# Two-layer hybrid trunk: delta-rule and retention heads issued in steps, with projections advanced K block by K block between them

## The chip, the cores and the metric

One core of one Trainium2 chip runs the whole program. The metric is device microseconds for one execution. Order on each engine is fixed when the program is built: TensorE, VectorE, ScalarE, GpSimd and the queue of SP (which issues nearly all DMAs) each work through their own list, and wait on semaphores for one another.

## The reference: what is computed

There are 512 latent tokens, 256 context tokens, a width of 2048 and two layers. In float32, each layer does the following:

```python
h  = rmsnorm(x, norm_w) * (1 + scale) + shift      # scale, shift, gate from silu(c) @ ada_w + ada_b
z  = h @ w_in                                      # one projection, split by columns
ret = silu(z_rg) * rmsnorm(retention(rope(z_rq), rope(z_rk), z_rv))       # 4 heads of 128, both directions
q, k, v = silu(conv5(z_q, z_k, z_v));  q, k = l2norm(q), l2norm(k)
gdn = silu(z_gg) * rmsnorm(gated_delta_rule(q, k, v, g, beta))            # 4 heads of 128, both directions
mla = silu(z_mg) * attention(z_cq, z_ckv, z_kr)                           # 8 heads, low-rank q and kv
x  = x + gate * (concat(ret, gdn, mla) @ w_out)
```

The context tokens go through the same weights and read only context. In the second layer their output isn't needed, so most projections there are for the latents alone. The delta rule works on six chunks of 128 tokens per head and direction: a triangular inverse per chunk, then a chain of six dependent steps that carries a 128x128 state.

## The kernel before, in words

Each layer has three phases. Phase A projects the normalised input (tiles `hs`, 16 K blocks, each as a high and a low fp32r part) into all branches and runs the delta-rule and retention heads. Phase B is the attention, phase C the output projection with the residual.

A projection of 128 columns (`proj`, L290) loads its weights in tiles of four K blocks (`load_w`, tile `raw`, 5 buffers), splits them on ScalarE (`wh`, L227) and VectorE (`wl`, L228; 4 buffers each) and runs three matmuls of 512 latent columns into PSUM tile `zl` per K block, and three of 256 context columns into `zc` where the context is needed. PSUM tag "z" has three buffers. `ada_job` runs once in the middle of a projection: it advances the modulation vectors for later, with products on ScalarE (`ada_p`, L470) and sums on GpSimd (`ada_a`, L472).

What comes after a projection is of several kinds. `gate` (L614) applies SiLU and stores to DRAM (`gate_d`, L621), `latent` (L625) stores the attention's compressed inputs, `ret_raw` and `ret_v` (L942, L950) store retention's q, k and v (`ret_d`), and `conv_in` (L733) does the five-tap convolution on VectorE (L747) and SiLU, and leaves its result in a tile for the head.

`gdn_head` (L752) does, in order: project and convolve q, its sums of squares (L763); project and convolve k, turn it to token order (`knp`, L657), normalise, turn back (`ktp`); project and convolve v, turn it (`vnp`); decays `et` and `es`; the chunks' inverses by rounds of small float16 matmuls and VectorE operations (L841 to L891); the chain of six steps in both directions (L900 to L938); `out_norm` (L666). The work tiles come from shared tags, among them "t" with five buffers and "h" with five.

`ret_head` (L968) loads a retention head's q, k, v, applies the rotary tables, builds decay tables, and goes over six chunks: scores, a multiplication on VectorE, a split, and a weighted sum into `racc` (L1033).

A list of all other projections (`fill`, L1052) is cut in eight (`nf`), and each piece is traced behind one head. The tile framework orders each engine's instructions by a planning run with modelled durations: whatever is ready, the one traced first goes first; weight loads and splits are traced with high priority. So projections traced behind a head stand, in TensorE's list, in the gaps that the plan sees in the head.

```python
            fill = cq + gg[1:2] + ckv + gg[2:3] + rr[0] + gg[3:] + rr[1] + rr[2] + rr[3] + mg
            nf = [7, 6, 4, 5, 3, 3, 4, 4]
            for i, n in enumerate(nf):
                (gdn_head if i < 4 else ret_head)(*((i, gs) if i < 4 else (i - 4,)))
                for f in fill[sum(nf[:i]):sum(nf[:i + 1])]:
                    f()
```

The first four projections of a layer (`C_KR` and q, k, v of delta head 0) are done earlier by `first_groups` and only picked up in phase A.

Of the kernel before, what the change touches and what calls it, by code (L numbers as in the profile page):

```python
# [44 lines left out]
RSCALE = 1024.0  # L45

# [55 lines left out]
def trunk(  # L102
# [206 lines left out]

    FIRST = (C_KR, C_GDN, C_GDN + 512, C_GDN + 1024)  # L310
# [41 lines left out]
    def pair_groups(l, cols, hs, need_ctx):  # L352
# [54 lines left out]
    ret_d = [[[dr.tile([P, NT], F32, name=f"ret_d{l}_{h}_{w}") for w in range(3)] for h in range(4)] for l in range(DEPTH)]  # L407
    g_d = [dr.tile([48, P], F32, name=f"g_d{l}") for l in range(DEPTH)]
# [194 lines left out]
    def phase_a(l, hs):  # L603
        last = l == DEPTH - 1
        parB = par[l, 1]
        if True:
# [7 lines left out]
            def gate(c0, j):  # L614
                lo_ctx = not last
                zl, zc = proj_in(l, (c0), hs, lo_ctx)
# [8 lines left out]
            def latent(c0, j, need_ctx):  # L625
                kind = 0 if j < 6 else 1
                zl, zc = proj_in(l, (c0), hs, need_ctx)
# [38 lines left out]
            def out_norm(o, lo, wcol, j, fill_v=mean_eps):  # L666
# [5 lines left out]
                scale_tokens(sq, o, r, c0)  # L672
                m = pm("ot")
# [5 lines left out]
            def kr_ab():  # L679
                zl, zc = proj_in(l, C_KR, hs, True)  # L680
# [52 lines left out]
            def conv_in(dst, c0, grp, need_ctx):  # L733
                zl, zc = proj_in(l, c0, hs, need_ctx)
# [4 lines left out]
                w = lambda j: parB[:, 12 * j + grp:12 * j + grp + 1]  # L739
# [10 lines left out]
                silu_mul(dst[:, lo:NT], y[:, lo:NT], e[:, lo:NT])  # L750

            def gdn_head(h, gs):  # L752
                be, gcol, egl, ekd, nbe = gs
                qT = pt("qT")
                qlo = NX if last else 0
                conv_in(qT, C_GDN + h * P, h, not last)
                qv = tiny("qv")
                sq = mk("lsq")
                S.activation(out=sq[:, qlo:NT], in_=qT[:, qlo:], func=AF.Square)
                m = pm("ss")  # L760
                c0 = qlo // P
                for n in range(c0, NCH):
                    T.matmul(m[:, n:n + 1], lhsT=sq[:, n * P:(n + 1) * P], rhs=ones[:, 0:1], start=True, stop=True)  # L763
                V.tensor_scalar(out=qv[:, c0:], in0=m[:, c0:NCH], scalar1=EPS, scalar2=EPS * HD, op0=ALU.add, op1=ALU.mult)
                kr = mk("kr")
                conv_in(kr, C_GDN + 512 + h * P, 4 + h, True)
# [5 lines left out]
                m = pm("ktp")  # L772
                turn(m, kn, 0)
                S.copy(kT, m[:, :NT])
                vT = mk("vT")
                conv_in(vT, C_GDN + 1024 + h * P, 8 + h, True)
                if h == 0:
                    gate(C_GDN + 1536, 4)

# [4 lines left out]
                S.copy(vn, m[:, :NT])  # L784
                on = pt("on")
                qch = range(2, NCH) if last else range(NCH)
# [50 lines left out]
                for n_ in range(5):  # L837
# [7 lines left out]
                    else:  # L845
# [525 lines left out]
```

## Time and profile before

| | us |
|---|---|
| median of 3 runs | 3240.17 (3236.0 to 3242.21) |
| profiled execution, first to last instruction (its span; no other time of it is given) | 3227.6 |
| TensorE busy | 3066.9 |
| VectorE busy | 2026.6 |
| ScalarE busy | 1643.0 |
| GpSimd busy | 695.7 |

The profile is of one execution. Times in its views are microseconds from the first instruction. PE is TensorE, PEld its weight loads, DVE VectorE, ACT ScalarE, POOL GpSimd; `SPq` is SP's queue. L763 is line 763 of the kernel. A matmul's recorded duration overlaps the next one's, so the distance between starts tells the rate. PEclk is the granted clock of TensorE: 1.00 is 2.4 GHz, and in a stretch's mean a lower figure is a share of time at 1.2 GHz. Phase A of layer 0 lies at about 200 to 1300 us, that of layer 1 at about 1960 to 2800; delta head 1 of layer 0 lies at about 440 to 660.

### The profile page before, as it was taken

The numbers are of one execution on the slowest core, as the hardware profiler recorded it, in microseconds if no ns is written. First come the engines' busy times: TensorE is split into PE (matmuls) and PEld (weight loads), VectorE is DVE, ScalarE is ACT, GpSimd is POOL, SyncE is SP. The second block draws the span as 40 slices with busy tenths as digits, with TensorE's granted clock in tenths as the row PEclk, the third lists the DMA queues.
The fourth block names the chain that finished last, engine by engine and source line by source line (L and its number), as shares of the span: only waits on it lengthen the run. The fifth ranks groups of instructions, "written<-read, shape, count | busy, mean of one in ns | idle before, by whom it ended". The sixth has DMA issues, their size and how long they took to land.

```text
span 3227.6 us, 50779 instructions
## 1 busy us (share of the span) xinstructions
PE 3066.9 (95%) x18925; PEld 2583.6 (80%) x18925; DVE 2026.6 (63%) x3524; ACT 1643.0 (51%) x3492; POOL 695.7 (22%) x487
## 2 busy tenths in 40 slices
PE   7998988989989999999999998899999999999998
PEld 3466877878778878899888887688898888888887
DVE  3259558568577666666743266867585767766634
ACT  3256555554654666544665566442425235644533
POOL 0026344444442554000246503200000000000000
PEclk9999999989999999999999999999999999999999
DMA  9763333433424555511465443321423256512444
GB/s 308 217 198 111 113 111 93 130 87 92 123 86 134 154 162 159 159 48 50 141 208 152 142 112 108 108 72 55 108 58 95 75 152 178 153 51 64 133 118 128
DMA packets 496654, 399.22 MB, mean 124 GB/s; under 512 B 45366, under 2 KB 433046, under 8 KB 496406
## 3 DMA queue, kind: packets, MB, share of 16 engines
q1 hardware_dynamic: 496310, 395.95, 41.5%
q8 instruction: 148, 2.42, 0.3%
q14 instruction: 100, 0.82, 0.1%
q0 software_dynamic: 96, 0.02, 0.0%
HBM read 340.90 MB, written 54.97 MB: 123 GB/s over the span
## 4 chain that ended last, share of the span: by engine, by line
PE 58%; DVE 4%; ACT 3%; issue 1%; DMA 1%; POOL 0%; SPq 0%; ACTq 0%; DVEq 0%; POOLq 0%
PE zl L284 20%; PE zlc L284 10%; PE zc L286 5%; PE vz L267 4%; PE sc L1153 3%; PE zlc L286 2%; PE oacc L1212 2%; PE zt L275 2%; PE ptp L1205 1%; PE racc L1033 1%; PE f L284 1%; DVE wl L228 1%; DVE cy L747 1%; ACT ada_p L470 0%; PE chain L912 0%
## 5 line engine op out<-in xcount | busy, mean ns | idle before, releaser
L472 POOL TENSOR_TENSOR ada_a<-ada_a,ada_p 128x512 f32<-128x512 f32 x480 | 693.8, 1445 | 1355.0 <-ACT ada_p L470 1259.7
L228 DVE TENSOR_TENSOR wl<-raw,wh 128x512 fp32r<-128x512 f32 x632 | 471.2, 753 | 198.2 <-ACT wh L227 155.3
L284 PE MATMUL zl<-hh,wh 128*128 128x512 f32 (+1 forms) x1440 | 584.9, 407 | 6.4 <-ACT wh L227 2.9
L284 PE MATMUL zl<-hh,wl 128*128 128x512 f32 (+1 forms) x1440 | 583.0, 405 | 6.6 <-DVE wl L228 6.6
L284 PE MATMUL zl<-hl,wh 128*128 128x512 f32 (+1 forms) x1440 | 584.6, 406 | 1.0 <-DVE hl L228 1.0
L470 ACT ACTIVATE ada_p<-araw,const_f 128x256 f32<-128x256 f32 x960 | 422.9, 499 | 86.9 <-DMA araw<-in_ada_w_dram 57.2
L227 ACT CAST wh<-raw 128x512 fp32r<-128x512 f32 x632 | 368.7, 601 | 72.8 <-PE vz L267 18.2
L284 PEld LDWEIGHTS zl<-hh,wh 128*128 128x128 f32 (+1 forms) x1440 | 275.2, 191 | 75.0 <-issue 9.1
L284 PEld LDWEIGHTS zl<-hh,wl 128*128 128x128 f32 (+1 forms) x1440 | 275.2, 191 | 67.6 <-DVE wl L228 8.1
L284 PEld LDWEIGHTS zl<-hl,wh 128*128 128x128 f32 (+1 forms) x1440 | 275.8, 192 | 63.5 <-DVE hl L228 4.2
L286 PE MATMUL zc<-hh,wh 128*128 128x256 f32 (+1 forms) x960 | 279.6, 291 | 3.2 <-ACT ce L372 1.8
L286 PE MATMUL zc<-hh,wl 128*128 128x256 f32 (+1 forms) x960 | 279.0, 291 | 0.0
L286 PE MATMUL zc<-hl,wh 128*128 128x256 f32 (+1 forms) x960 | 278.5, 290 | 0.0
L286 PEld LDWEIGHTS zc<-hh,wh 128*128 128x128 f32 (+1 forms) x960 | 184.2, 192 | 12.5 <-issue 4.7
L286 PEld LDWEIGHTS zc<-hl,wh 128*128 128x128 f32 (+1 forms) x960 | 184.4, 192 | 6.9 <-issue 5.0
L286 PEld LDWEIGHTS zc<-hh,wl 128*128 128x128 f32 (+1 forms) x960 | 184.1, 192 | 5.1 <-issue 4.6
L284 PE MATMUL zlc<-mh,wl 128*128 128x512 f32 x448 | 176.7, 395 | 0.0
L284 PE MATMUL zlc<-mh,wh 128*128 128x512 f32 x448 | 175.8, 392 | 0.0
L284 PE MATMUL zlc<-ml,wh 128*128 128x512 f32 x448 | 175.4, 391 | 0.0
L747 DVE SCALAR_TENSOR_TENSOR cy<-cz,const_f,cy 128x511 f32<-128x511 f32 (+3 forms) x176 | 145.7, 882 | 28.0 <-ACT cy L740 27.7
L284 PEld LDWEIGHTS zlc<-mh,wh 128*128 128x128 f32 x448 | 84.1, 188 | 19.0 <-issue 1.2
L284 PEld LDWEIGHTS zlc<-ml,wh 128*128 128x128 f32 x448 | 84.0, 187 | 18.3
(1250 smaller groups left out, 6426.0 us busy)
## 6 DMA issues: line engine op xcount, KB each, us to landing
raw<-in_w_in_dram SPq DMA_DIRECT2D x368, 256.0 KB, 3.7
araw<-in_ada_w_dram SPq DMA_DIRECT2D x256, 256.0 KB, 3.2
raw<-in_w_out_dram SPq DMA_DIRECT2D x144, 256.0 KB, 4.1
ar<-in_ada_w_dram SPq DMA_DIRECT2D x128, 256.0 KB, 4.8
x_d<-xt SPq DMA_DIRECT2D x32, 384.0 KB, 5.4
raw<-in_w_in_dram SPq DMA_DIRECT2D x72, 128.0 KB, 3.2
ret_d<-rw SPq DMA_DIRECT2D x20, 384.0 KB, 4.0
rz<-ret_d SPq DMA_DIRECT2D x20, 384.0 KB, 4.3
```

What stands on the lines that cost most here:

```text
L227: S.copy(hi, src)
L228: V.tensor_tensor(out=lo, in0=src, in1=hi.bitcast(F32), op=ALU.subtract)
L267: T.matmul(z[:, 256 * i:256 * i + 256], lhsT=x_[:, (j + i) * P:(j + i + 1) * P], rhs=w, start=first and k == 0 and i == 0, stop=end and k ...
L275: T.matmul(z, lhsT=w, rhs=xx[:, a:b], start=own and first and k == 0, stop=own and last and k == nk - 1)
L284: T.matmul(zl[:m], lhsT=w, rhs=xx[:, NX:], start=st, stop=sp)
L286: i = T.matmul(zc[:m, :NX], lhsT=w, rhs=xx[:, :NX], start=st and zc_open, stop=sp and zc_open)
L470: S.activation(out=pr[:, v], in_=raw[:, i, :], func=AF.Copy, scale=cs32[:, 2 * k + v:2 * k + v + 1])
L472: G.tensor_tensor(out=acc, in0=acc, in1=pr, op=ALU.add)
L747: V.scalar_tensor_tensor(out=y[:, a_:b_], in0=z[:, a_ + o:b_ + o], scalar=w(j), in1=y[:, a_:b_], op0=ALU.mult, op1=ALU.add)
L1033: T.matmul(acc[:, :NL], lhsT=a[:, sl], rhs=b[:, :NL], start=st and i == 0, stop=sp and i == NCH - 1)
L1153: T.matmul(m[:, po:po + n], lhsT=a[:, qs], rhs=b[:, ko:ko + n], start=i == 0, stop=i == len(ops) - 1)
L1212: T.matmul(acc[:, os], lhsT=a[:, sl], rhs=b[:, js], start=j == 0 and n == 0, stop=j == nk - 1 and n == 2)
```

## The change

Projections of phase A become tasks: Python generators that trace one K block and then give back its length in microseconds (`STEP_US`; 2.1 for `ret_v`). `pump(us)` inside `gdn_head`, `ret_head` and `out_norm` advances the first unfinished tasks by that much, so that these matmuls are traced between the steps of the head, ahead of the head's next step. `need(key)` advances the list until all tasks of a key are done. Weights are taken four K blocks at a time. The convolutions of a delta head (`conv_task`) become tasks as well, placed one head ahead in the list, in the order k, v, q; their results are stored in DRAM (`conv_d`) and loaded by `gdn_load` ahead of the previous head's output norm. Inside a head, the two directions are traced step by step side by side. The number of projections, taps and `ada_job` calls is the same.

```diff
+STEP_US = (0.7, 1.05)
...
+    def proj_steps(segs, xs, m, need_ctx):
+        nk = len(xs)
+        zl = pz("zl")
+        zc = pz("zc") if need_ctx else None
+        for k0 in range(0, nk, 4):
+            ws = load_w(segs, k0, 4, m)
+            for j in range(4):
+                pmm(ws[j:j + 1], xs, k0 + j, nk, m, zl, zc)
+                yield STEP_US[bool(need_ctx)]
+            if k0 == 4:
+                ada_job()
+        return zl, zc
...
-    def pair_groups(l, cols, hs, need_ctx):
...
+                yield 4 * STEP_US[bool(need_ctx)]
...
-        return proj(segs, hs, m, need_ctx, True)
+        return (yield from proj_steps(segs, hs, m, need_ctx))
...
+                pump(6)
...
+                zl, zc = ready.pop((l, C_KR))
...
+            def conv_task(h, which):
+                need = which > 0 or not last
+                zl, zc = yield from proj_in(l, C_GDN + 512 * which + h * P, hs, need)
                 z = ev("cz")
-                lo = 0 if need_ctx else NX
...
-                silu_mul(dst[:, lo:NT], y[:, lo:NT], e[:, lo:NT])
-
-            def gdn_head(h, gs):
+                silu_mul(z[:, lo:NT], y[:, lo:NT], e[:, lo:NT])
+                dma(out=conv_d[l][h][which][:, lo:], in_=z[:, lo:])
+
+            def gdn_load(h):
+                qlo = NX if last else 0
+                kr, vT, qT = mk("kr"), mk("vT"), pt("qT")
+                for w, t in ((1, kr), (2, vT), (0, qT)):
+                    lo = qlo if w == 0 else 0
+                    dma(out=t[:, lo:], in_=conv_d[l][h][w][:, lo:])
+                return kr, vT, qT
+
+            def gdn_head(h, gs, loaded, pump):
...
-                conv_in(kr, C_GDN + 512 + h * P, 4 + h, True)
+                qch = range(2, NCH) if last else range(NCH)
+                kr, vT, qT = loaded
...
-                if h == 0:
-                    gate(C_GDN + 1536, 4)
-
+                pump(4)
...
+                qv = tiny("qv")
+                sq = mk("lsq")
+                S.activation(out=sq[:, qlo:NT], in_=qT[:, qlo:], func=AF.Square)
+                pump(4)
+                m = pm("ktp")
+                turn(m, kn, 0)
+                S.copy(kT, m[:, :NT])
+                pump(2)
+                ss = pm("ss")
+                for n in qch:
+                    T.matmul(ss[:, n:n + 1], lhsT=sq[:, n * P:(n + 1) * P], rhs=ones[:, 0:1], start=True, stop=True)
+                V.tensor_scalar(out=qv[:, c0:], in0=ss[:, c0:NCH], scalar1=EPS, scalar2=EPS * HD, op0=ALU.add, op1=ALU.mult)
...
+                pump(4)
...
+                pump(4)
...
+                pump(8)
...
+                        pump(1)
...
+                    pump(3)
...
+                    ms = []
...
+                        ms.append(vt)
+                        pump(1)
+                    for d in both:
                         mx = pm("xp")
                         for sl in sls:
-                            T.matmul(mx[:, sl], lhsT=X[d][:, sl], rhs=vt[:, sl], start=True, stop=True)
+                            T.matmul(mx[:, sl], lhsT=X[d][:, sl], rhs=ms[d][:, sl], start=True, stop=True)
                         V.tensor_tensor(out=Xt[d], in0=Xt[d], in1=mx[:, :NT], op=ALU.subtract)
+                        pump(1)
...
+                        pump(1)
...
+                pump(2)
...
+                    if step:
+                        pump(1)
+                    for d, (n, cl, sl) in enumerate(info):
+                        T.matmul(pp[d][:, P:2 * P], lhsT=Xs[d][:, sl], rhs=rs[d], start=True, stop=True)
...
+                    pump(1)
+                    S2 = [None] * 2
+                    for d, (n, cl, sl) in enumerate(info):
...
+                    pump(1)
+                ahead = gdn_load(h + 1) if h < 3 and need("conv", h + 1) else None
                 out_norm(on, qlo, parB[:, 71:72], 4 + h, lambda ss: V.scalar_tensor_tensor(
-                    out=ss, in0=ss, scalar=1.0 / HD, in1=qv[:, c0:], op0=ALU.mult, op1=ALU.add))
+                    out=ss, in0=ss, scalar=1.0 / HD, in1=qv[:, c0:], op0=ALU.mult, op1=ALU.add), pump)
+                return ahead
...
-                    for j, z in enumerate(zs):
-                        tok_mm(z, hs, ws, 2 * j, k0, KD)
+                    for i in range(4):
+                        for j, z in enumerate(zs):
+                            tok_mm(z, hs, ws[i:i + 1], 2 * j, k0 + i, KD)
+                        yield 2.1
...
+                pump(8)
...
+                    pump(3)
...
+                pump(2)
                 m = pm("on")
                 turn(m, o, qlo // P)
-                out_norm(m, qlo, parB[:, 70:71], h)
-
+                out_norm(m, qlo, parB[:, 70:71], h, pump=pump)
...
+            tasks = {}
+
+            def task(name, g):
+                tasks[name] = g
+
+            def advance(name):
+                us = next(tasks[name], None)
+                if us is None:
+                    del tasks[name]
+                return us or 0
+
+            def pump(us):
+                while us > 0 and tasks:
+                    us -= advance(next(iter(tasks)))
+
+            def need(*key):
+                while any(n[:len(key)] == key for n in tasks):
+                    pump(0.1)
+                return True
+
+            def pair_gate(j):
+                yield from pair_steps(l, (C_MG + j * P, C_MG + (j + 1) * P), hs, not last)
+                for i in (j, j + 1):
+                    yield from gate(C_MG + i * P, 8 + i)
+
+            conv = lambda h: [task(("conv", h, w), conv_task(h, w)) for w in (1, 2, 0)]
+            cq = lambda a, b: [task(("cq", j), latent(C_CQ + j * P, j, not last)) for j in range(a, b)]
+            ckv = lambda a, b: [task(("ckv", j), latent(C_CKV + j * P, 6 + j, True)) for j in range(a, b)]
+            gg = lambda h: task(("gg", h), gate(C_GDN + 1536 + h * P, 4 + h))
+            rr = lambda h: [task(("rr", h, w), ret_raw(h, w)) for w in range(2)]
+            rv = lambda h: task(("rr", h, "v"), ret_v(h))
+            rg = lambda h: task(("rr", h, "g"), gate(C_RET + 1536 + h * P, h))
+            mg = lambda a, b: [task(("mg", j), gate(C_MG + j * P, 8 + j)) for j in range(a, b)]
             gs = kr_ab()
-            cq = [lambda j=j: latent(C_CQ + j * P, j, not last) for j in range(6)]
-            ckv = [lambda j=j: latent(C_CKV + j * P, 6 + j, True) for j in range(4)]
-            rr = [[lambda h=h, w=w: ret_raw(h, w) for w in range(2)] +
-                  [lambda h=h: ret_v(h)] * (1 - h % 2) + [lambda h=h: gate(C_RET + 1536 + h * P, h)] for h in range(4)]
-            gg = [lambda h=h: gate(C_GDN + 1536 + h * P, 4 + h) for h in range(4)]
-            mg = [lambda j=j: gate(C_MG + j * P, 8 + j) for j in range(8)]
-            mg.insert(6, lambda: pair_groups(l, (C_MG + 6 * P, C_MG + 7 * P), hs, not last))
-            fill = cq + gg[1:2] + ckv + gg[2:3] + rr[0] + gg[3:] + rr[1] + rr[2] + rr[3] + mg
-            nf = [7, 6, 4, 5, 3, 3, 4, 4]
-            for i, n in enumerate(nf):
-                (gdn_head if i < 4 else ret_head)(*((i, gs) if i < 4 else (i - 4,)))
-                for f in fill[sum(nf[:i]):sum(nf[:i + 1])]:
-                    f()
+            conv(0)
+            need("conv", 0)
+            gg(0)
+            cq(0, 6)
+            conv(1)
+            gg(1)
+            ckv(0, 4)
+            conv(2)
+            gg(2)
+            rr(0)
+            rv(0)
+            conv(3)
+            gg(3)
+            rg(0)
+            rr(1)
+            rg(1)
+            rr(2)
+            rv(2)
+            rg(2)
+            rr(3)
+            rg(3)
+            mg(0, 6)
+            task(("mg", 6), pair_gate(6))
+            ahead = gdn_load(0)
+            pump(24)
+            for h in range(4):
+                need("gg", h)
+                ahead = gdn_head(h, gs, ahead, pump)
+            for h in range(4):
+                need("rr", h)
+                if h % 2:
+                    need("rr", h - 1)
+                ret_head(h, pump)
+            while tasks:
+                pump(1)
```

## Rows read from the trace of the kernel before

**Rows 1.** Profile page: the span, and busy time of each engine.

```profile
span 3227.6 us, 50779 instructions
...
PE 3066.9 (95%) x18925; PEld 2583.6 (80%) x18925; DVE 2026.6 (63%) x3524; ACT 1643.0 (51%) x3492; POOL 695.7 (22%) x487
```

**Rows 2.** Busy time by stretch, layer 0; columns in the first line.

```profile
core 0: us, PE busy (x) PEld busy (x) DVE busy (x) ACT busy (x) POOL busy (x), PEclk, DMA share, GB/s
200.00:440.00 240.00, 214.96 (x1395) 182.26 (x1395) 173.35 (x266) 145.58 (x327) 116.74 (x79) 0.96 0.45 134
440.00:510.00 70.00, 55.70 (x298) 47.64 (x296) 47.72 (x69) 42.89 (x91) 28.70 (x20) 0.90 0.24 66
660.00:730.00 70.00, 57.05 (x317) 49.45 (x316) 46.70 (x66) 39.39 (x85) 27.08 (x20) 0.88 0.25 72
880.00:950.00 70.00, 58.32 (x331) 49.44 (x331) 54.15 (x87) 43.11 (x95) 34.44 (x23) 0.91 0.21 61
440.00:1040.00 600.00, 537.98 (x3679) 466.66 (x3678) 410.76 (x655) 332.16 (x753) 248.64 (x174) 0.95 0.35 101
1040.00:1300.00 260.00, 248.61 (x1473) 213.91 (x1471) 174.02 (x221) 168.09 (x366) 122.06 (x82) 0.99 0.55 161
200.00:1300.00 1100.00, 1001.55 (x6542) 862.82 (x6541) 758.12 (x1140) 645.83 (x1444) 487.44 (x334) 0.96 0.42 123
1300.00:1600.00 300.00, 299.70 (x1955) 269.97 (x1953) 203.38 (x401) 151.19 (x307) 12.33 (x10) 1.00 0.31 91
```

**Rows 3.** Busy time by stretch, phase A of layer 1.

```profile
1960.00:2060.00 100.00, 82.50 (x400) 64.61 (x399) 82.70 (x138) 68.15 (x151) 44.27 (x30) 0.90 0.43 116
2060.00:2800.00 740.00, 735.00 (x4783) 627.57 (x4782) 514.47 (x982) 309.98 (x626) 0.00 (x0) 1.00 0.37 106
```

**Rows 4.** Waits of TensorE, 440:1040, largest first: us, times, longest.

```profile
PE knp L657 <- DVE kr L400: 15.9, 3, 5.6
PE ss L763 <- ACT lsq L759: 15.5, 3, 5.3
PE vtp L848 <- DVE vt L842: 8.0, 4, 2.9
PE ot L657 <- DVE osq L660: 4.7, 2, 3.3
```

**Rows 5.** Timeline of TensorE, 443:453: start, us, operation, idle before.

```profile
442.82 0.40 PE L284 MATMUL zl<-hl,wh 128*128 128x512 f32 x1
...
443.88 0.40 PE L284 MATMUL zl<-hl,wh 128*128 128x512 f32 x1
449.27 2.72 PE L763 MATMUL ss<-const_f,lsq 128*128 128x1 f32 x12 [4.99 <-ACT lsq L759]
...
452.20 0.63 PE L284 MATMUL zl<-hh,wl 128*128 128x512 f32 x1
```

**Rows 6.** Groups of VectorE by line, 200:1300; count, busy us, mean ns.

```profile
L228 DVE TENSOR_TENSOR wl<-raw,wh 128x512 fp32r<-128x512 f32 x180 | 166.5, 926 | 54.7 <-ACT wh L227 41.4 <-issue 7.3 <-POOL ada_a L472 3.5
L747 DVE SCALAR_TENSOR_TENSOR cy<-cz,const_f,cy 128x254 f32<-128x254 f32 (+1 forms) x96 | 92.4, 1022 | 10.7 <-ACT cy L740 10.7
```

**Rows 7.** Groups of VectorE by line, 2060:2800.

```profile
L228 DVE TENSOR_TENSOR wl<-raw,wh 128x512 fp32r<-128x512 f32 (+1 forms) x170 | 114.7, 680 | 28.9 <-ACT wh L227 28.7
L747 DVE SCALAR_TENSOR_TENSOR cy<-cz,const_f,cy 128x510 f32<-128x510 f32 (+3 forms) x60 | 35.3, 638 | 15.5 <-ACT cy L740 15.2
```

**Rows 8.** DMA issues on the page: count, KB, us to landing.

```profile
ret_d<-rw SPq DMA_DIRECT2D x20, 384.0 KB, 4.0
rz<-ret_d SPq DMA_DIRECT2D x20, 384.0 KB, 4.3
```

**Rows 9.** Waits of SP's queue, the largest.

```profile
SPq L621 <- DVE gz L400: 181.3, 24, 17.7
```

**Rows 10.** Busy time by stretch, head 1 of layer 0.

```profile
498.00:605.00 107.00, 95.76 (x743) 81.56 (x743) 81.76 (x154) 55.20 (x132) 42.81 (x30) 0.98 0.32 92
440.00:660.00 220.00, 197.20 (x1301) 168.38 (x1300) 144.59 (x228) 125.51 (x283) 95.88 (x67) 0.96 0.36 104
```

More of the change, by code (lines that the diff above doesn't have):

```diff
@@ L407, in trunk @@
     ret_d = [[[dr.tile([P, NT], F32, name=f"ret_d{l}_{h}_{w}") for w in range(3)] for h in range(4)] for l in range(DEPTH)]
+    conv_d = [[[dr.tile([P, NT], F32, name=f"conv_d{l}_{h}_{w}") for w in range(3)] for h in range(4)] for l in range(DEPTH)]
     g_d = [dr.tile([48, P], F32, name=f"g_d{l}") for l in range(DEPTH)]
@@ L615, in gate @@
                 lo_ctx = not last
-                zl, zc = proj_in(l, (c0), hs, lo_ctx)
+                zl, zc = yield from proj_in(l, c0, hs, lo_ctx)
                 z, e = ev("gz"), ev("ge")
@@ L626, in latent @@
                 kind = 0 if j < 6 else 1
-                zl, zc = proj_in(l, (c0), hs, need_ctx)
+                zl, zc = yield from proj_in(l, c0, hs, need_ctx)
                 e = ev("ce")
@@ L876, in gdn_head @@
                 for it in range(2):
+                    Rs = []
                     for d in both:
@@ L899, in gdn_head @@
                 small = lambda name, tag, bufs: wk.tile([P, P], F32, name=name, tag=tag, bufs=bufs)
+                pump(2)
                 for step in range(NCH):
-                    for d in both:
-                        n, cl, end = orders[d][step], col(d), step == NCH - 1
-                        sl = sls[n]
-                        p_ = pc("chain") if d == 0 else pm("chain")[:, :512]
+                    end = step == NCH - 1
+                    info = [(orders[d][step], col(d), sls[orders[d][step]]) for d in both]
+                    pp, rs, vd, vnew = [None] * 2, [None] * 2, [None] * 2, [None] * 2
+                    for d, (n, cl, sl) in enumerate(info):
+                        pp[d] = pc("chain") if d == 0 else pm("chain")[:, :512]
@@ L905, in gdn_head @@
                         if step == 0:
[L906 removed]
+                            rs[d] = vn[:, sl]
                         else:
[L908 to L910 removed]
+                            T.matmul(pp[d][:, 0:P], lhsT=kT[:, sl], rhs=St[d], start=True, stop=True)
@@ L919, in gdn_head @@
-                            S.copy(vnew, p_[:, P:2 * P])
+                            vnew[d] = small("vnew", "svn", 2)
+                            S.copy(vnew[d], pp[d][:, P:2 * P])
+                    pump(1)
+                    S2 = [None] * 2
+                    for d, (n, cl, sl) in enumerate(info):
                         if not end:
-                            T.matmul(p_[:, 2 * P:3 * P], lhsT=kn[:, sl], rhs=vd, start=True, stop=True)
-                            S2 = small("St", "ss", 4)
+                            T.matmul(pp[d][:, 2 * P:3 * P], lhsT=kn[:, sl], rhs=vd[d], start=True, stop=True)
+                            S2[d] = small("St", "ss", 4)
@@ L944, in ret_raw @@
                 lo = 0 if need else NX
-                zl, zc = proj_in(l, C_RET + 512 * which + h * P, hs, need)
+                zl, zc = yield from proj_in(l, C_RET + 512 * which + h * P, hs, need)
                 z = ev("rw")
@@ L966, in ret_v, with ret_head @@
                     dma(out=ret_d[l][h + e][2], in_=o)
-            def ret_head(h):
+            def ret_head(h, pump):
                 qlo = NX if last else 0
@@ L1059, in phase_b @@
+            for h in range(4):
[4 more added lines that the diff above has]
+            while tasks:
+                pump(1)
     def phase_b(l):
```

58 lines of the change are left out of this document (20 added, 38 removed).

## The prediction

> **What bounds the kernel now.** I read the page's busy shares first: TensorE 95%, VectorE 63% [rows 1]. One busy engine at 95% sounds finished, so the next view is busy time by stretch, where the reader is to see two kinds of stretch. From 1300 to 1600 us TensorE is busy 299.70 of 300 us at full granted clock; from 200 to 1300, phase A of layer 0, it is busy 1001.55 of 1100 at a mean clock of 0.96 [rows 2]. A mean of 0.96 with the two levels 2.4 and 1.2 GHz means some 8% of that time at the lower one. I price a stretch as idle time plus (1 − clock) × length: 98.4 + 44 = about 142 us. Layer 1 runs the same code, but only its first 100 us look like that (17.5 idle, clock 0.90); its other 740 us are busy 735 [rows 3]. So at most some 170 us of the run can be won from order alone, and nearly all of it is in layer 0.
>
> The third view, TensorE's waits inside 440:1040 (heads 1 to 3 of the delta rule), names them: the transposes of k wait for the convolved `kr` (15.9 us in 3 waits), the sums of squares of q wait for `lsq` (15.5 in 3), then the small inverse waits for VectorE (8.0 in 4), and the output norm (4.7 in 2) [rows 4]. The timeline of one such wait shows the form: projection matmuls at full rate, 4.99 us of nothing, then the next matmuls at 0.63 us each where 0.40 was usual [rows 5]. Each head begins with convolutions of q, k and v one after another, and TensorE's queue has the consumer of the first standing ahead of projection work that could have run.
>
> Why only layer 0? A convolution tap on VectorE takes 1022 ns there and 638 in layer 1 after 2060 us, a weight split 926 against 680 [rows 6, 7]; GpSimd is busy 487.44 us in the first stretch and 0.00 in the second [rows 2, 3]. The projection order was interleaved with the head, but with too little work between dependent steps for these slower operations.
>
> The Trainium skill, GPSIMD Engine Reference, section Specifications, says that GpSimd shares its SBUF interfaces with VectorE and contends with instructions that have two SBUF inputs; these rows agree. The change leaves every GpSimd addition in place, so by that rule the waits inside the heads would stay (term 2 below at zero) and the sum would be 3184 us.
>
> **The change part by part.** Matmuls, taps and weight bytes stay the same. New are 24 stores and 24 loads of convolved q, k, v (`conv_d`), all on SP's queue.
>
> The step price first. Twelve projection matmuls, two K blocks with context, run from 442.82 in pairs some 0.35 us apart [rows 5], so a block (three pairs) is 1.05 us and a full projection 16 × 1.05 = 16.8 us. Summing the budgets in the diff, a delta head hands out 84 us before it asks for the next head's convolution and 6 in the output norm; a retention head 34. Following the task list in layer 0 with these numbers: before head 0 24 us; by the end of head 0 108, then `need` forces the list to 185 (three convolutions and a gate); head 1 ends at 319, head 2 at 454, head 3 at 544, the retention heads at 689 of about 790. So the list doesn't run dry there; in layer 1 (about 627 us, steps of 0.7 that overshoot each pump(1) by 0.4) it may end within the last retention head.
>
> Term 1, starts of heads 1 to 3 in layer 0 (440:510, 660:730, 880:950). Idle 14.3 + 12.95 + 11.68 = 38.9, clock 7.0 + 8.4 + 6.3 = 21.7, together 60.6 [rows 2]. The two leading waits are 31.4 of the idle [rows 4]. With k projected first, then v, q, a gate and the output norm, some 16.8 + 16.8 + 6 + 16.8 = 56 us of matmuls lie between the k projection and the turn of k; its convolution needs 8 taps × 1.02 = 8.2 [rows 6], some 8 more for SiLU, and store and load 4.0 + 4.3 [rows 8], 25 in all. It is hidden for k; for q, projected last, 6 + 16.8 + 10 and the first transposes, about 37 us, cover the same 25. Bounds: 0 (the wait only moves to the load) to 60.6. I take 40: the row for the waits, and a part of the clock.
>
> Term 2, inside these heads. 440:1040 has 62.0 idle and 30 of clock [rows 2]; less term 1: 23.1 and 8.3. Now 4 to 8 us of projection stand between dependent steps of the setup, about 4 in each round of the inverse. Also both directions are issued before either is used, but tag "h" has five buffers, four of them held by X and Xt, so the second `vt` or `R` still waits for the first one's reader: nothing gained, nothing lost. Bounds −10 (projection evacuations now precede the head's next step in VectorE's queue) to 31; I take 14, not quite half, since slower taps stay.
>
> Term 3, head 0 of layer 0 (200:440): 25.0 idle and 9.6 clock [rows 2]. Its convolutions still come first and in series, and now go through DRAM: 8.3 us more before k can be turned [rows 8], under pump(24). Bounds −8 to 34.6; I take 6.
>
> Term 4, retention heads (1040:1300): 11.4 idle, 2.6 clock [rows 2]; pump(3) stands ahead of each weighted sum. Bounds −5 to 14; I take 5.
>
> Term 5, layer 1: first 100 us 17.5 idle and 10 clock, where I take 5 (bounds −8 to 27.5 as in term 3); of the rest at most 5 can be won [rows 3], and up to 15 lost if the list ends early; I take 0.
>
> Cost at nothing: SP's queue. Each store waits for VectorE while weight loads stand behind it. The gate stores already do so, 181.3 us in 24 waits, the longest 17.7 [rows 9], and waits of TensorE for `wl` don't appear among the leading ones [rows 4]: five raw buffers and four split pairs, each 4.2 us of matmuls, cover it. If a store blocked for over 20 us, that cover would be gone and TensorE would stand for the excess.
>
> Sum: 40 + 14 + 6 + 5 + 5 = 70 us. The profiled execution is known by its span, 3227.6 [rows 1]; the median of the runs lies 12.6 above it. 3227.6 − 70 + 12.6 = 3170 us.
>
> **The rivals.** Everything closes: terms 1, 2 and 4 whole, half of 3 and 5: 60.6 + 31.4 + 14 + 17 + 14 = 137, 3103 us. For it speaks that 1300:1600 and layer 1's heads run at this density; against, that both are stretches with little or no GpSimd.
>
> The wait only moves. The scheduler already filled gaps with projections, and what ended late were VectorE's operations, which do not get faster. TensorE then stands at the first use of the loaded k, at the sums of squares, and in the inverse; only the clock part of term 1 is won back, or nothing: 3220 to 3246, say 3236.
>
> Slower: VectorE's order. A convolution's evacuation, taps and SiLU, about 10 us, now stand in VectorE's queue in the middle of another head's serial steps, where they stood before the head. Work it out for layer 0: a head's serial part took from about 498 to 605 us, 107 us, and VectorE was busy 144.59 of the 220 us period [rows 10]. The new period has 134 us of projections and about 37 of its own matmuls (220 less 22.8 idle, 9 clock and 9 × 16.8 projections), 171. VectorE would be 85% busy, and 107 + 30 = 137 leaves 34 us of slack. The sign turns where each head's serial part grows by more than that, which the work buffers could do: a convolution needs two of the five "t" buffers while the two directions' decays hold four. Then layer 0 gains nothing, and layer 1's four dense heads lose: 8 us each is 3270.
>
> The Trainium skill, TensorE: Matmul & The Clock Gate, section "Architectural detail: the array is 16× 32×32, not 1× 128×128", says VectorE and ScalarE are strictly first in, first out. By that a projection's evacuation that waits holds up the delta step behind it; no row here shows that case, and it would give this rival's 3270.
>
> **How the numbers follow.** My forecast (3140 to 3200) 47%; everything closes (below 3140) 17%; the wait moves (3200 to 3246) 21%; slower 15%. What the measurement can tell from no change is 0.2%, 6.5 us. Faster: 47 + 17 + 11 of the 21 = 75%; within 9%; slower 16%. The bounds of the terms add to 173 won and 46 lost, 3067 to 3286; I cut at 3100 and 3255, leaving some 6% below and 11% above.
>
> **What would show it.** In the profile after: no waits of the turns of k and the sums of squares in heads 1 to 3 of layer 0; granted clock near 1.00 there; the head period near 171 us instead of 220; phase A of layer 0 some 65 us shorter, layer 1 equal within 10. Term 2 is wrong if the inverse's waits stay at their sum, term 1 if the first use of the loaded tiles waits by as much. The prediction as a whole falls if TensorE's idle time in phase A of layer 0 stays near 98 us, or if layer 1's dense stretch opens.

## The result, and the profile after

The changed kernel takes 3264.19 us (median of 4 runs, 3257.63 to 3267.47), the kernel before, run beside it, 3239.68; the ratio is 1.0076, 95% interval 1.0060 to 1.0091. It is 0.8% slower, where 2% faster was forecast, and the time lies outside the range. The profiles differ by more than the medians: 3265.7 against 3227.6 us, since the profiled execution of before is a quick one. So a difference of some 10 us between two profiles is read as real only where several runs show it.

The page, then the stretches of [rows 2, 3] and the list's end; columns as there.

```profile
span 3265.7 us, 50966 instructions
...
PE 3078.7 (94%) x18925; PEld 2588.1 (79%) x18925; DVE 2057.9 (63%) x3524; ACT 1651.7 (51%) x3492; POOL 705.4 (22%) x487
```

```profile
200.00:440.00 240.00, 207.22 (x1326) 175.95 (x1325) 167.92 (x260) 138.44 (x299) 107.26 (x73) 0.94 0.46 134
440.00:510.00 70.00, 56.57 (x320) 49.50 (x319) 54.18 (x75) 45.20 (x109) 30.95 (x21) 0.90 0.39 121
660.00:730.00 70.00, 52.32 (x309) 45.15 (x309) 55.14 (x88) 47.35 (x115) 34.61 (x23) 0.88 0.49 149
880.00:950.00 70.00, 59.62 (x403) 51.45 (x404) 55.89 (x99) 45.12 (x112) 33.30 (x23) 0.88 0.44 130
440.00:1040.00 600.00, 541.61 (x3779) 471.86 (x3778) 421.19 (x664) 344.38 (x794) 259.77 (x182) 0.95 0.40 118
1040.00:1300.00 260.00, 242.97 (x1408) 208.60 (x1407) 186.78 (x236) 162.37 (x363) 121.17 (x80) 0.98 0.58 175
200.00:1300.00 1100.00, 991.80 (x6509) 856.41 (x6508) 775.88 (x1159) 645.19 (x1454) 488.20 (x334) 0.96 0.46 135
...
1960.00:2060.00 100.00, 84.16 (x391) 65.91 (x390) 77.11 (x130) 69.11 (x152) 48.74 (x33) 0.90 0.52 144
2060.00:2800.00 740.00, 727.44 (x4748) 623.22 (x4747) 485.83 (x939) 295.24 (x592) 0.00 (x0) 0.99 0.38 107
2800.00:2840.00 40.00, 29.69 (x100) 19.14 (x100) 32.01 (x54) 19.77 (x41) 0.00 (x0) 0.79 0.69 207
```

The reader is to see that the dense stretch did not come. TensorE is idle 108.2 us in 200:1300, 98.4 before. By phase, before and then after: phase A of layer 0 grew by 5 us, that of layer 1 by 21, and phase B of layer 1 by 10; the rest is equal within 1. So nearly all of the loss is in layer 1, and layer 0 merely failed to win its 65. (Phase B of layer 1 takes 240 to 243 us in nine of the profiles of this case and 231 to 233 in the other seven, so these 10 us are real.)

```profile
201.00:1343.00 1142.00, 1043.55 (x6783) 899.29 (x6782) 790.25 (x1187) 665.32 (x1484) 486.93 (x334) 0.96 0.43 125
...
1962.00:2790.00 828.00, 805.50 (x5126) 682.26 (x5125) 587.24 (x1100) 368.17 (x758) 42.98 (x29) 0.99 0.38 107
...
2790.00:3021.00 231.00, 229.56 (x1451) 204.07 (x1450) 160.81 (x316) 115.74 (x229) 0.00 (x0) 1.00 0.24 71
```

```profile
201.00:1348.00 1147.00, 1038.71 (x6777) 896.76 (x6777) 796.78 (x1189) 665.98 (x1486) 487.24 (x333) 0.96 0.45 133
...
1969.00:2818.00 849.00, 813.68 (x5124) 687.51 (x5124) 572.87 (x1087) 371.61 (x762) 44.29 (x29) 0.97 0.39 111
...
2818.00:3059.00 241.00, 236.13 (x1449) 206.37 (x1449) 171.16 (x327) 116.59 (x227) 0.00 (x0) 0.98 0.27 78
```

TensorE's waits, 440:1040, against [rows 4]:

```profile
PE ot L673 <- ACT ada_p L486: 26.3, 2, 13.2
PE zc L287 <- DVE gz L386: 8.8, 1, 8.8
PE ada_q L516 <- ACT ada_e L513: 4.8, 1, 4.8
PE vtp L874 <- DVE vt L867: 4.1, 5, 2.4
```

The waits of `knp` and `ss` (31.4 us) are gone; the transposes of the output norm stand 26.3 us in two waits instead. The timeline of the first, on TensorE, VectorE and ScalarE (start, us, operation, idle before):

```profile
474.68 0.40 PE L285 MATMUL zl<-hl,wh 128*128 128x512 f32 x1
488.19 1.51 PE L673 MATMUL ot<-const_f,osq 128*128 128x128 f32 x6 [13.11 <-ACT ada_p L486]
489.36 0.56 PE L287 MATMUL zc<-hh,wh 128*128 128x256 f32 x1
```

```profile
464.82 7.42 DVE L765 SCALAR_TENSOR_TENSOR cy<-cz,const_f,cy 128x254 f32<-128x254 f32 x6 [2.42 <-ACT cy L758]
472.16 1.77 DVE L229 TENSOR_TENSOR wl<-raw,wh 128x512 fp32r<-128x512 f32 x1
473.86 2.17 DVE L765 SCALAR_TENSOR_TENSOR cy<-cz,const_f,cy 128x254 f32<-128x254 f32 x2
...
486.12 1.92 DVE L676 TENSOR_TENSOR osq<-on,nss 128x768 f32<-128x768 f32 x1
```

```profile
476.12 0.84 ACT L407 ACTIVATE ce<-cy 128x768 f32<-128x768 f32 x1 [6.42 <-DVE cy L765]
...
482.14 0.31 ACT L665 ACTIVATE osq<-on 128x128 f32<-128x128 f32 x1 [0.52 <-DVE cz L415]
```

Head 0's norm begins only at 482.14: the forced q convolution of head 1 (taps to 476.0, SiLU to 482.1) stands ahead of it on both engines. The "ada_p" that is named as the releaser is a modulation job's scaling after the norm's squares; the chain is taps, SiLU, squares, scale.

### The profile page after: what moved, and what is told of

It reads as the page before. It is cut to its first block, busy times and chain, and to the rows that moved or that the text cites. A ratio compares the mean times of both kernels' runs of the same rounds, so it can differ in the third digit from the quotient of the medians.

```text
span 3265.7 us, 50966 instructions
## 1 busy us (share of the span) xinstructions
PE 3078.7 (94%) x18925; PEld 2588.1 (79%) x18925; DVE 2057.9 (63%) x3524; ACT 1651.7 (51%) x3492; POOL 705.4 (22%) x487
## 4 chain that ended last, share of the span: by engine, by line
PE 53%; DVE 4%; ACT 3%; DMA 1%; issue 1%; SPq 0%; POOL 0%; ACTq 0%; DVEq 0%; POOLq 0%
PE zl L285 17%; PE zlc L285 9%; PE zc L287 5%; PE vz L268 4%; PE sc L1262 3%; PE zlc L287 2%; PE oacc L1321 2%; PE zt L276 2%; PE ptp L1314 1%; PE f L285 1%; DVE cy L765 1%; DVE wl L229 1%; PE racc L1086 1%; DMA raw<-in_w_in_dram 0%; ACT wh L228 0%
## 5 line engine op out<-in xcount | busy, mean ns | idle before, releaser
L488 POOL TENSOR_TENSOR ada_a<-ada_a,ada_p 128x512 f32<-128x512 f32 x480 | 703.5, 1466 | 1351.9 <-ACT ada_p L486 1266.6
L229 DVE TENSOR_TENSOR wl<-raw,wh 128x512 fp32r<-128x512 f32 x632 | 486.8, 774 | 326.1 <-ACT wh L228 297.6
L285 PE MATMUL zl<-hh,wh 128*128 128x512 f32 (+1 forms) x1440 | 599.4, 417 | 4.5 <-ACT hh L228 2.2
```

What stands on the lines that cost most here:

```text
L229: V.tensor_tensor(out=lo, in0=src, in1=hi.bitcast(F32), op=ALU.subtract)
L285: T.matmul(zl[:m], lhsT=w, rhs=xx[:, NX:], start=st, stop=sp)
L488: G.tensor_tensor(out=acc, in0=acc, in1=pr, op=ALU.add)
```

## The experiments

First theory N: the norm was queued behind forced convolutions. (A convolution is forced where `need` advances the list until it is done.) Rivals were V (VectorE's order inside the heads) and M (the wait moves again). "Ideal" in the expectations is the 20th percentile of the interval from one matmul's start to the next, by shape. All ratios are to the kernel before, run beside the variant.

**e1: the norm first.**

```
-ahead = gdn_load(h + 1) if h < 3 and need("conv", h + 1) else None
 out_norm(on, ..., pump)
-return ahead
+return gdn_load(h + 1) if h < 3 and need("conv", h + 1) else None
```

> Changed kernel with out_norm ahead of the forced convolutions of the next head and their loads. Theory N (the loss is the output norm of a delta head, whose squares and scale stand in ScalarE's and VectorE's queues behind the taps and SiLU of the next head's q convolution, so that the transposes `ot` stop TensorE and its clock falls): the `ot` waits of heads 0 to 2 and the half-clock stretches behind them go (13.7, 16.7 and 9.4 us above the mean in layer 0, about 14 us in layer 1), the end of layer 1 stays: 3215 us (3203 to 3230). Rival V (VectorE's order inside the heads costs, wherever the norm stands): 3258 to 3268 us. Rival M (the norm's wait only moves on, to the next head's first transposes `knp`, because the loads are issued later): 3250 us, with waits of over 8 us at `knp`.

3253.63 us, 1.0061 (1.0035 to 1.0088). TensorE's waits, 440:1040:

```profile
PE ktp L673 <- DVE kn L676: 22.6, 3, 10.6
PE knp L673 <- ACT gz L387: 9.4, 1, 9.4
...
PE vnp L794 <- ACT gz L387: 4.2, 1, 4.2
PE ot L673 <- DVE osq L676: 2.8, 1, 2.8
```

The norm's 26.3 us became 36.2 at the next head's transposes (`ktp`, `knp`, `vnp`), and the interval overlaps that of the change. In layer 0, N names the place, not the cause; M holds here, in its time and in its wait at `knp`.

**e7: more cover ahead of `ot` in layer 0.**

```
-pump(6)
+pump(24 if j in range(4, 8) and not last else 6)
```

> Changed kernel with 24 us of tasks instead of 6 between the norm's scale and the transposes `ot` of layer 0's four delta heads; nothing changes place in VectorE's and ScalarE's queues before it. Theory N: 18 us more cover hides the late squares and scale of layer 0: minus 30 to 40 us, 3229 us (3222 to 3240). Rival V: 3258 to 3268 us. Rival M: as N here.

3266.46 us, 1.0086 (1.0070 to 1.0101): nothing won, a time in V's range. N falls for layer 0. M had priced the same gain here and misses it too, but a wait moved again: in 200:1345 `ot` stands 14.4 us instead of 30.7, and `ktp`, 1.1 in the change, has

```profile
PE ktp L673 <- DVE kn L676: 14.8, 3, 6.0
```

**e2: smaller budgets in layer 1.**

```
 def pump(us):
+    us *= 0.93 if last else 1.0
```

> Changed kernel with the advance budgets of layer 1 multiplied by 0.93, so that some 20 us of projection tasks are left when the last retention head is done. Theory L (part of the loss, 18 to 20 us, is that layer 1's list of tasks is empty before the last retention head): 3264 - 15 to 20 = 3247 us (3243 to 3252), the gap between the last projection matmul and phase B's first (19 us in the changed kernel) below 5 us. Rival V (all of the loss is inside the heads): 3260 to 3268 us.

3255.0 us, 1.0055 (1.0035 to 1.0074): 9 us less than the change, where L expected 15 to 20, and the two intervals overlap, so even the 9 are not told from none. The list lasted, but phase B of layer 1 still took 242 us; e5 shows why.

**e5: the convolutions earlier in the list** (the list written on one line).

```
-gg(0) cq(0, 6) conv(1) gg(1) ckv(0, 4) conv(2) gg(2) rr(0) rv(0) conv(3) gg(3) rg(0)
+gg(0) cq(0, 2) conv(1) gg(1) cq(2, 3) conv(2) gg(2) cq(3, 4) conv(3) gg(3) cq(4, 6) ckv(0, 4) rr(0) rv(0) rg(0)
```

> Changed kernel with another order of the tasks: the three convolutions of head h+1 stand two to three tasks further ahead, so that they are finished inside head h and are not forced at its end. Theory N: no convolution stands ahead of the norm, so its waits go in both layers (40 and 14 us), and with fewer forced tasks layer 1's list lasts to the end (18 us): 3195 us (3185 to 3215). Rival V: the same number of taps stands in the middle of other heads' serial steps, earlier by two tasks: 3255 to 3270 us. Rival M: without forced projections at the seams the next head's start is bare again: 3240 to 3270 us with waits at `knp` and `ss`.

3240.61 us, 1.0011 (1.0001 to 1.0021). All taps now lie in the middle of other heads' serial steps, and neither layer's phase A is longer for it, so V falls. It is 24 us faster than the change, and the gain is in layer 1: its phase A takes 832 us (849) and its phase B 231 (241). There N was right in part: the `ot` waits in 2060:2840, 15.4 us in the change, are 6.3 up to e5's phase B. Layer 0's phase A stays at 1143 us, where N expected 40 us less: its waits spread over the steps (the inverse's `vtp` 37.5 us in 200:1345, 19.9 in the change). In the 20 us from layer 1's phase B start (after, then e2, then e5) TensorE is busy

```profile
2818.00:2838.00 20.00, 16.61 (x51) 11.16 (x52) 18.67 (x29) 8.39 (x13) 0.00 (x0) 0.76 0.86 251
```

```profile
2810.00:2830.00 20.00, 13.59 (x50) 8.15 (x48) 19.81 (x32) 14.36 (x26) 0.00 (x0) 1.00 0.98 294
```

```profile
2797.00:2817.00 20.00, 20.00 (x126) 18.14 (x125) 13.34 (x25) 14.09 (x27) 0.00 (x0) 1.00 0.44 126
```

Between the last norm's transposes and phase B's first matmul lie 0.7 us in the change, 2.6 in e2 and 33.5 in e5 (16.3 in the kernel before). So the tasks left over in e2 cover the last norm, not phase B's loads and splits; the order of e5 leaves more and covers both.

**e8 and e11: larger budgets in layer 0's heads** (e11 with the order of e5).

```
-ahead = gdn_head(h, gs, ahead, pump)
+ahead = gdn_head(h, gs, ahead, pump if last else lambda us: pump(1.35 * us))
```

> Changed kernel with the advance budgets of layer 0's four delta heads multiplied by 1.35 (by whole K blocks that is about 145 us of projection in a head instead of 88, and next to nothing is forced at its end). Moving the norm alone gave 10 us, since waits of 22.6 us at `ktp` and 13 us at `knp` took its place. Theory C (between two serial steps of a head there is less projection work than the step's latency on VectorE and ScalarE takes; 94 us above the ideal issue times inside the four heads and 60 us at their seams): both fall by half or more, layer 0's phase A from 1147 to 1080 to 1105 us, the time 3215 us (3195 to 3225). Rival Q (every projection brings its own evacuation, taps and SiLU into the two queues, so the waits stay as large, only elsewhere): layer 0's phase A 1135 to 1155 us, the time 3250 to 3272 us.

> The earlier order of the convolutions (which alone gave 3241 us) with the budgets of layer 0's delta heads multiplied by 1.35. Theory C: minus 40 to 60 us against the order alone: 3190 us (3175 to 3205), below the kernel before. Rival Q: 3230 to 3250 us.

3273.2 us, 1.0109 (1.0094 to 1.0124), and 3228.68, 0.9978 (0.9968 to 0.9987). C falls for e8: layer 0's phase A was 1137 us, and its list was empty 38 us before its end. With the earlier order the larger budgets won 12 us of the 40 to 60. The waits still followed.

**e9 and e10: 15/16 of the modulation jobs left out**, in the changed kernel and in the one before. A job multiplies blocks of a modulation weight on ScalarE (`ada_p`) and adds them up on GpSimd (`ada_a`).

```
-for j in range(2):
+for j in range(1 if qd == 0 else 0):
...
+    if k:
+        continue
```

> Changed kernel in which the modulation jobs keep one of their 16 K blocks (15/16 of their loads, ScalarE scalings and GpSimd additions are left out; their closing matmuls stay). To be read against the kernel before with the same left out. Theory G (the jobs' ScalarE and GpSimd work is what makes the steps of layer 0's heads and of layer 1's first head late: 24 to 34 us above the ideal issue times a head there, 9 to 14 us in the other heads of layer 1, which have no jobs): 3264 - 60 to 90 = 3190 us, and the loss of the change falls from 25 to below 10 us. Rival (the jobs matter little, layer 0's heads are slow by their own VectorE work): 3240 to 3262 us, loss as before.

> The kernel before with the same 15/16 of the modulation jobs left out. Theory G: 3240 - 50 to 80 = 3175 us. Rival: 3215 to 3238 us.

3096.49 us, 0.9566 (0.9550 to 0.9582), and 3090.51, 0.9548 (0.9534 to 0.9563). Twice what G expected. The jobs cost the changed kernel 168 us and the one before 147, and the loss between them is 0.18% (0.0018, with the two half-widths added in squares ±0.0022): not told from none. Phase A of layer 0 and of layer 1, changed kernel, then before:

```profile
199.00:1203.00 1004.00, 996.85 (x6783) 870.04 (x6782) 621.83 (x1188) 407.23 (x818) 0.00 (x0) 1.00 0.38 111
...
1820.00:2647.00 827.00, 803.83 (x5127) 680.09 (x5125) 552.02 (x1086) 347.65 (x703) 0.00 (x0) 0.99 0.39 110
```

```profile
201.00:1224.00 1023.00, 1005.91 (x6775) 875.95 (x6775) 625.08 (x1186) 410.06 (x816) 0.00 (x0) 0.99 0.35 99
...
1842.00:2653.00 811.00, 802.25 (x5125) 680.21 (x5124) 566.51 (x1100) 351.29 (x701) 0.00 (x0) 0.99 0.38 105
```

Without jobs the change does in layer 0 what it is for (7 us idle, 19 us shorter). It still loses 16 in phase A of layer 1, whose list runs out and whose `ot` waits are 15.7 us (2.5 in the kernel before), and 10 in its phase B (242 against 232). So the two times are equal because a gain and a loss balance; the loss in layer 1 does not come from the jobs.

**e14 and e15: which half of a job.** e14 leaves out GpSimd's additions, e15 ScalarE's scalings.

```
e14: -    if k:
     -        G.tensor_tensor(out=acc, in0=acc, in1=pr, op=ALU.add)
e15: ...                              (k > 0: no S.activation)
     +        G.tensor_tensor(out=acc, in0=acc, in1=raw, op=ALU.add)
```

> Changed kernel with the modulation jobs' GpSimd additions left out, the loads and ScalarE's scalings kept (leaving out 15/16 of all three gave 3096 us, 168 us less). Theory P (the additions make VectorE's SBUF operations longer: X<-vt 1044 to 1317 ns in layer 0's heads against 554 without them): 3120 us (3096 to 3150), X<-vt at 550 to 560 ns. Rival S (ScalarE's 500 ns scalings stand ahead of the serial steps in its queue): 3220 to 3255 us.

> Changed kernel with the modulation jobs' scalings on ScalarE left out (but for the first K block), the loads and GpSimd's additions kept (they add the unscaled weights). Theory P: 3230 us (3200 to 3255), X<-vt still 900 to 1300 ns in layer 0's heads. Rival S: 3125 us (3096 to 3160).

3117.69 us, 0.9640 (0.9626 to 0.9655), and 3245.87, 1.0032 (1.0016 to 1.0049). The additions are worth 147 of the 168 us, the scalings 18; S falls. (X<-vt is at 865 ns in e15, just under P's 900 to 1300.) That GpSimd holds up ScalarE through the jobs' shared tiles is no rival either: in e15 ScalarE has hardly any part in a job, and the time stays. One VectorE operation of the inverse in layer 0's four heads shows how; ns min/median/max, for the kernel before, the changed one, and e14:

```profile
L833 DVE TENSOR_TENSOR X<-vt,const_f x40: 544/559/1653, 289.7 to 973.1; 128x768 f16<-128x768 f16 x40
```

```profile
L858 DVE TENSOR_TENSOR X<-vt,const_f x40: 548/1060/1685, 291.0 to 955.1; 128x768 f16<-128x768 f16 x40
```

```profile
L856 DVE TENSOR_TENSOR X<-vt,const_f x40: 547/552/559, 276.7 to 857.1; 128x768 f16<-128x768 f16 x40
```

Mostly the operation takes 550 or about 1640 ns: it goes through alone or stands for an addition. One pair of the changed kernel:

```profile
530.34 1.66 POOL L488 TENSOR_TENSOR ada_a<-ada_a,ada_p 128x512 f32<-128x512 f32 x1 [5.68 <-ACT ada_p L486]
530.78 1.65 DVE L858 TENSOR_TENSOR X<-vt,const_f 128x768 f16<-128x768 f16 x1
```

Of the 40 operations, 16 before and 21 after began while an addition still had over 0.1 us to run, and every one of these 37 ended 0.41 to 0.42 us after that addition. The others took 544 to 561 ns. The mean is 910 ns before, 1097 after (first two lines below are of before, then of after, 200:1300); the operation of the second line, which reads PSUM, doesn't change.

```profile
L833 DVE TENSOR_TENSOR X<-vt,const_f 128x768 f16<-128x768 f16 x40 | 35.0, 910 | 0.4
...
L861 DVE TENSOR_TENSOR vt<-vtp,const_f 128x768 f16<-128x768 f32 x16 | 15.2, 950 | 3.0 <-PE vtp L859 3.0
```

```profile
L858 DVE TENSOR_TENSOR X<-vt,const_f 128x768 f16<-128x768 f16 x40 | 43.0, 1097 | 0.4
...
L889 DVE TENSOR_TENSOR vt<-vtp,const_f 128x768 f16<-128x768 f32 x16 | 15.0, 950 | 4.5 <-PE vtp L887 2.7 <-POOL ada_a L488 1.7
```

The Trainium skill, SBUF — State Buffer, section "SBUF: two separate sides", says that VectorE and GpSimd share a pair of ports, that it goes to whichever instruction starts first for its whole length, and that a VectorE operation with two SBUF inputs asks for it. The two lengths, the 37 ends and the unchanged PSUM line agree.

Why more in the changed kernel? A job comes with each projection. The serial parts of layer 0's four heads (from some 6 us ahead of `knp` to the last `chain`, summed over four windows each) held, before and after:

```profile
sum 513.00, PE 453.15 PEld 392.25 DVE 394.03 ACT 294.12 POOL 220.34; mean PE 113.29 PEld 98.06 DVE 98.51 ACT 73.53 POOL 55.09
```

```profile
sum 586.00, PE 537.15 PEld 468.13 DVE 432.53 ACT 337.41 POOL 272.72; mean PE 134.29 PEld 117.03 DVE 108.13 ACT 84.35 POOL 68.18
```

The 244 additions from the first of these windows to the last, gaps included, take as long in both kernels:

```profile
L472 POOL TENSOR_TENSOR ada_a<-ada_a,ada_p 128x512 f32<-128x512 f32 x244 | 354.1, 1451 | 427.0 <-ACT ada_p L470 367.6 <-PE chain L921 12.4 <-ACT nry L375 9.2
```

```profile
L488 POOL TENSOR_TENSOR ada_a<-ada_a,ada_p 128x512 f32<-128x512 f32 x244 | 352.3, 1444 | 436.7 <-ACT ada_p L486 395.5 <-ACT nry L391 18.3 <-DVE nrt L394 11.5
```

So of the same additions, 273 us lie beside the serial steps instead of 220. In part that is because these stretches themselves are longer, 586 us against 513; GpSimd's share of them is 47% against 43%. What it does to VectorE can be added up by tile in layer 0's phase A, each kernel against itself without jobs: the operations of the projections (splits, taps, evacuations, SiLU) are longer by 92 us before and 79 after, all others, most of them the heads', by 72 and 97.

**e13 and e16: the jobs held back** during the first three delta heads of each layer and made up for later (18 of them in layer 0's phase B), in the changed kernel and in the one before. No work is left out.

```
 def ada_job():
+    if ada_state["hold"]:
+        return
...
+ada_state["hold"] = True           # from the start of phase A until three heads are through
+ada_state["b"] = 18 * (l == 0)     # phase B: one job behind each of 18 projections
```

> Changed kernel, alone with the modulation jobs held back during the first three delta heads of each layer and made up for in layer 0's phase B and the later heads; all the work is done. Theory G: layer 0's phase A falls from 1147 to 1070 to 1095 us, the others stay within 10 us: 3210 us (3190 to 3230), so below the kernel before. Rival: 3250 to 3272 us.

> The kernel before with the modulation jobs held back in the same way as in the run that holds them in the changed kernel (3217 us): none while the first three delta heads of a layer and the tasks listed behind them run, made up for in layer 0's phase B and later; all the work is done. With the jobs reduced to 1/16 the change lost 6 us instead of 25 (20 us won in layer 0's phase A, 16 us lost in layer 1's). Theory G (the change loses because its steps lie beside the jobs): with the jobs out of the way in both, the kernel before gains less than the changed one did (47 us): 3205 us (3195 to 3215), so that the loss of the change is 0 to 20 us. Rival (the hold helps both alike): 3237 - 47 = 3190 us (3184 to 3194), the loss of the change stays at 25.

3216.64 us, 0.9940 (0.9922 to 0.9958), and 3223.39, 0.9971 (0.9957 to 0.9985). The hold wins some 44 to 47 us in the changed kernel, some 9 to 12 in the one before, and the sign turns: with jobs held, the change is 0.31% (±0.23) faster. G has the direction; e16's 3223 is above its range, so the hold was worth less in the kernel before than G said. Phase A of layer 0, e13 and then e16:

```profile
201.00:1259.00 1058.00, 1013.68 (x6697) 882.00 (x6697) 693.24 (x1175) 517.36 (x1104) 227.18 (x154) 0.97 0.40 120
```

```profile
199.00:1284.00 1085.00, 1020.07 (x6707) 887.12 (x6706) 710.33 (x1177) 532.08 (x1126) 240.73 (x164) 0.97 0.37 109
```

There the change is 27 us shorter, and 89 shorter than without the hold, of which layer 0's phase B, where held jobs run, takes back 28 (307 against 279) and layer 1's phase A 17. In layer 1 the change still loses: 866 against 846 in phase A, 242 against 231 in phase B.

**e12 and e17: toward a better version.** e12 is e11 with the hold. e17 is e5 with the hold over all four delta heads and 14 jobs in phase B.

> The earlier convolutions with the larger budgets (3229 us), and no modulation jobs during layer 0's first three delta heads and layer 1's first three; the jobs left out there run in 18 of phase B's projections of layer 0, and in the later heads. Theory G (the jobs are dear because they run beside the serial steps of the delta heads): layer 0's three heads lose 20 to 30 us each of the time above ideal, phase B of layer 0 gains up to 10 us: 3229 - 50 = 3180 us (3160 to 3205). Rival (a job costs the same wherever it stands): 3220 to 3240 us.

> The earlier order of the convolutions with its own budgets (3241 us), and the modulation jobs held back through all four delta heads of each layer; 14 of them in layer 0's phase B. Theory G: the four heads of layer 0 lose 20 to 25 us each of the time above ideal, none of the two layers' lists runs dry (the run with larger budgets had a gap of 38 us at the end of layer 0's phase A), and layer 1's last head keeps its 11 us above ideal instead of 21: 3165 us (3150 to 3185). Rival (jobs that are crowded into the retention heads and phase B cost there what they saved): 3195 to 3220 us.

3202.08 us, 0.9903 (0.9888 to 0.9918): the larger budgets empty layer 0's list 38 us early, as in e8. And 3176.27 us, 0.9815 (0.9800 to 0.9829): e17 beats both kernels. Layer 0's phase A takes 1037 us (1142 before), its phase B 301 (278). In the stretch of its four heads TensorE is idle 8 us of 528:

```profile
231.00:759.00 528.00, 520.08 (x3826) 452.65 (x3825) 389.43 (x789) 217.78 (x459) 9.46 (x7) 0.99 0.30 86
```

## Why the prediction was wrong

**The bottleneck** was read rightly: layer 0's waits, and GpSimd as what sets the layers apart. Two steps failed. The first is how the contention was used: "slower taps stay" made it a fixed length of each operation. The taps did stay (1022 ns before, 1006 after), but how much an operation is stretched depends on what lies beside what, and the change moves the jobs, which ride on the projections, into the serial steps. The prediction's list of what is added to a head had projections and their evacuations, but not the job that each brings. With the jobs out of the way layer 0's phase A gains 19 us (e9 against e10) or 27 (e13 against e16); with them it loses 5, where 65 won were forecast. The second is layer 1 (term 5): it was to win 5 and lost 31, and 26 still without jobs, by a norm that stands behind forced convolutions and a list that ended early. That made the change slower.

**Term 1** (40 won) failed. The named waits went as said: 56 us of matmuls cover the convolved k. The output norm was counted as cover, not as a chain with a consumer of its own, which now stands behind the next head's convolutions. Idle and clock in the three windows are 13.4 + 17.7 + 10.4 and 7.0 + 8.4 + 8.4, together 65.3, where [rows 2] had 60.6; e1 shows the same wait one place further. Heads 1 to 3 begin (`knp`) 202 and 195 us apart, where 171 was forecast and the kernel before had 223 and 201.

**Term 2** (14 won): 440:1040 as a whole has 58.4 us idle and 30 of clock, 62.0 and 30 before. With nothing won at the starts, some 4 + 5 us were won inside. **Term 3** (6 won): idle 32.8 and clock 14.4, against 25.0 and 9.6: 12.6 lost, past its bound of −8. **Term 4** (5 won): 17.0 and 5.2 against 11.4 and 2.6: 8 lost, past −5. These stretches are fixed in time and hold somewhat different work in the two kernels, so the sizes of terms 3 and 4 are rough: layer 0's whole phase A is 5 us longer.

**Term 5** (5 won, up to 15 lost if the list ends early) was mis-sized: 31 lost. The list did end, in the last retention head. 2800:2838 lost 6.9 + 3.4 idle and 3.2 + 4.8 of clock, 18 us, half of it at phase B's start, which the working left out. In 2060:2800 the norm's waits and the clock behind them add 15 (12.6 idle and a clock of 0.99, against 5.0 and 1.00).

**SP's queue at nothing** held: its longest wait for the new stores was 19.7 us, just under the 20 that the prediction named, and TensorE waited 2.7 us for `wl` in 440:1040.

**The rivals.** "The wait only moves" had the mechanism, though it looked for the wait at the loaded k and in the inverse, and with 3236 left out layer 1. "Slower: VectorE's order" had nearly the time, 3270, and its shape: nothing won in layer 0, a loss in layer 1's dense heads. Its reason was taps in the middle of serial steps, and e5, which puts all of them there, refutes it. But the order did cost at the seams: with GpSimd still, e9 has 15.7 us of `ot` waits in layer 1, and e5's order gives most of layer 1's loss back. "Everything closes" needs GpSimd still: only then is layer 0's phase A idle for 7 us (e9). The Trainium skill's rule of the GPSIMD Engine Reference, section Specifications, on shared SBUF interfaces was cited for 3184 as a loss of term 2 alone; by e14 the additions are worth 147 us here.

**Left open:** why the jobs cost the kernel before 147 us, though its serial parts hold fewer of them, is not split further; and how layer 1's loss divides between the list's end (18 by idle and clock in one profile, 9 or nothing by e2) and the norm (15 in the same profile) is known only to within those. e2, which changes layer 1 alone, does not repair it; e5, which does, changes the order in layer 0 too.

## What to carry to other kernels

List everything that a moved step brings with it, side jobs on idle-looking engines too, and ask what each will lie beside in its new place. A wait that goes says little until the next consumer on the same in-order queues has been named; here it went from `knp` to `ot` and back without the time changing. When waits move and don't shrink, leave out whole resources one by one: e9 and e14 told more of layer 0 than the four runs that moved the wait. And compare phase by phase before explaining a difference: here the gain that failed to come and the loss that came lay in different layers.

## What had not been expected of the hardware

A VectorE operation with two SBUF operands beside GpSimd's additions had two lengths and few between: 550 ns or about 1640, for additions of 1444 ns in the mean. An operation of the inverse that began under a running addition ended 0.41 to 0.42 us after it, 37 times of 37. Taps went from 612 ns (e9, without jobs) to 1006, weight splits from 678 to 894, means over 200:1300. GpSimd was busy 22% of the span, and its additions were worth 4.5% of the time.
